# Splitting the first loads of a matmul with RMS norm over both hardware DMA queues, with the first PSUM moves on two engines and 8 warm-up matmuls

## The chip, the cores and the metric

The kernel runs on one core of one Trainium2 chip. The metric is the device time of one execution in microseconds; a median over several executions is given. Each comparison was made with runs of the kernel before on the same chip.

The engines of the core are PE (TensorE, matmul), DVE (VectorE), ACT (ScalarE), POOL (GpSimd) and SP (the sync engine). SP and ACT each issue on a hardware DMA queue; GpSimd issues on a software queue. All queues feed the same 16 DMA engines.

## The reference

```python
# a: 2048 x 2048, b: 2048 x 2048, gamma: 2048, all fp32
x = np.matmul(a, b)
rms = np.sqrt(np.mean(x ** 2, axis=-1, keepdims=True) + eps)
return (gamma * x / rms).astype(np.float32)
```

## The kernel before

A head of four row blocks of A (512 rows) is computed with plain matmuls while B streams in; the other row blocks use a Strassen-like scheme with seven products on B's sums. The contraction has 16 tiles of 128, taken in 8 pairs. Pair 0 is loaded in fp32 on the hardware queues and cast on chip; pairs 1 to 7 come on GpSimd's queue, which casts to bf16 on the way (fp32 read, bf16 written). "B tile 0" and "B tile 1" below are the two tiles of pair 0.

```python
nc.sync.dma_start(out=a0f, in_=a[0:HB * P, 0:W2].rearrange("(r p) k -> p r k", p=P))   # A of pair 0
for t in range(2):                                                                     # B tiles 0 and 1
    nc.scalar.dma_start(out=b0f[t], in_=b[t * P:(t + 1) * P, 0:HALF])
# ...
def load_head(kp):                       # a later pair: its A, then its B
    nc.gpsimd.dma_start(out=ah(kp), in_=a[0:HB * P, kp * W2:(kp + 1) * W2].rearrange(...))
    load_b(0, kp)
# ...
load_head(1)
identity_f = consts.tile([P, P], FP32, name="identity_f")
make_identity(nc, identity_f)
for kp in range(2, 4):
    load_head(kp)
# ...
for _ in range(11):                      # warm-up matmuls on zeros
    nc.tensor.matmul(warm_bank, warm[:, 0:P], warm[:, 0:CH], start=True, stop=True)
# ...
def transpose_first():
    # eight fp32 transposes of A's pair 0 into two PSUM banks, then:
    for t in range(2):
        cast_first = [lambda: nc.vector.tensor_copy(out=raw[0][0][:, t, :CH], in_=b0f[t][:, :CH]),
                      lambda: nc.scalar.copy(out=raw[0][0][:, t, CH:], in_=b0f[t][:, CH:])]
        move = [lambda h=h: nc.vector.tensor_copy(
            out=head_at[:, t, 2 * h:2 * h + 2, :], in_=view[t][:, 2 * h:2 * h + 2, :])
            for h in range(2)]
        for work in (cast_first + move if t == 0 else move + cast_first):
            work()
# ...
for kp in range(KP):                     # the head: 14 matmuls of 512 columns a pair, 8 transposes, 2 more
    # loads of a later pair; transposes of pair kp + 1; matmuls of pair kp
```

In pair 0 PE does 7 matmuls on tile 0, 5 on tile 1, the transposes of pair 1's A, and the last 2 on tile 1.

Of the kernel before, what the change touches and what calls it, by code (L numbers as in the profile page):

```python
# [17 lines left out]
def kernel(  # L18
# [13 lines left out]
    nc = tc.nc  # L32
    P = 128
    M, K = a.shape
    _, N = b.shape
    KT = K // P
    KP = KT // 2
    W2 = 2 * P
    MB = M // P
    CH = 512  # L40
    NCH = N // CH
    HALF = N // 2
    HB = 4
# [15 lines left out]
    head_at = consts.tile([P, KT, HB, P], BF16, name="head_at")  # L59
    raw = [[consts.tile([P, 2, HALF], BF16, name=f"b_{j}_{kp}") for kp in range(KP)]  # L60
           for j in range(2)]
# [4 lines left out]
    a0f = early[:, 0:2048].bitcast(FP32).rearrange("p (r k) -> p r k", r=HB)  # L66
    b0f = [early[:, 2048 + t * 2048:2048 + (t + 1) * 2048].bitcast(FP32) for t in range(2)]
# [21 lines left out]
        return (at_even, at_odd)[(mb // 2) % 2][:, mb % 2]  # L89


    nc.sync.dma_start(out=a0f, in_=a[0:HB * P, 0:W2].rearrange("(r p) k -> p r k", p=P))
    for t in range(2):
        nc.scalar.dma_start(out=b0f[t], in_=b[t * P:(t + 1) * P, 0:HALF])

    def ah(kp):
        return ah_slot[(kp - 1) % NAH]
# [36 lines left out]


    warm_bank = ps_a.tile([P, CH], FP32, name="acc")
    for _ in range(11):
        nc.tensor.matmul(warm_bank, warm[:, 0:P], warm[:, 0:CH], start=True, stop=True)

    gamma_sb = consts.tile([P, N], FP32, name="gamma_sb")  # L140
# [2 lines left out]
    def transpose_first():  # L143
        bank = [ps_t.tile([P, CH], FP32, name="tbank"), ps_a.tile([P, CH], FP32, name="acc")]
        view = [b.rearrange("p (r m) -> p r m", r=HB) for b in bank]
        for t in range(2):
            for r in range(HB):
                nc.tensor.matmul(view[t][:, r, :], a0f[:, r, t * P:(t + 1) * P], identity_f,
                                 is_transpose=True, start=(r == 0), stop=(r == HB - 1))
        for t in range(2):  # L150
            cast_first = [lambda: nc.vector.tensor_copy(out=raw[0][0][:, t, :CH],
                                                        in_=b0f[t][:, :CH]),
                          lambda: nc.scalar.copy(out=raw[0][0][:, t, CH:], in_=b0f[t][:, CH:])]
            move = [lambda h=h: nc.vector.tensor_copy(
                out=head_at[:, t, 2 * h:2 * h + 2, :], in_=view[t][:, 2 * h:2 * h + 2, :])
                for h in range(2)]
            for work in (cast_first + move if t == 0 else move + cast_first):
                work()

    def transpose_head(kp):  # L160
        bank = ps_t.tile([P, CH], FP32, name="tbank")
# [236 lines left out]
    for r in range(HB):  # L398
        x_tile(r, 0)
    transpose_first()  # L400
    for kp in range(KP):
        if kp + 4 < KP:
# [334 lines left out]
```

## Time and profile before

| | before |
|---|---|
| time, median of 3 runs | 224.7 us |
| span of the profiled run | 222.6 us |
| PE busy | 211.1 us, 95% |
| A of pair 0 landed | 6.43 us |
| B tile 0, tile 1 landed | 5.12, 8.67 us |
| B of pairs 1, 2, 3, 4 landed | 12.34, 16.04, 19.87, 24.65 us |

The landings are the times in the trace at which a load's semaphore was complete, from the span's start. First the page: the busy share of PE and its granted clock (what the trace records of the TensorE clock, as a share of full speed), both in tenths, in 40 slices of 5.6 us each.

```profile
PE   7899999999999999999999999999999999999950
...
PEclk9999999999999999999999999999999999999997
```

The chain of work that ended last, in order of time (start, duration, what), the lines that matter:

```profile
7.18 17.47 DMA b<-in_b_dram
24.64 0.04 issue
24.69 1.67 PE acc L350 x7
...
69.41 140.08 PE acc L279 x648
```

PE runs unbroken from 24.69 us to 209.5 us. Before that the chain is a load: the B of pair 4. So the length of the program is that landing, plus a fixed run of PE, plus a tail.

The timeline of the first pair (start, duration, engine, line, operation, how many; in brackets the idle time before it and what ended it):

```profile
5.14 0.62 ACT L153 CAST b<-early 128x512 bf16<-128x512 f32 x1 [2.17 <-DMA early<-in_b_dram]
5.14 0.73 DVE L151 CAST b<-early 128x512 bf16<-128x512 f32 x1 [1.32 <-DMA early<-in_b_dram]
...
7.03 0.60 PE L148 MATMUL acc<-identity_f,early 128*128 128x128 f32 x4
7.23 0.76 DVE L154 CAST head_at<-tbank 128x256 bf16<-128x256 f32 x2 [1.36 <-PE tbank L148]
7.71 2.76 PE L350 MATMUL acc<-b,head_at 128*128 128x512 bf16 x12
7.90 0.75 DVE L154 CAST head_at<-acc 128x256 bf16<-128x256 f32 x2
8.69 0.62 ACT L153 CAST b<-early 128x512 bf16<-128x512 f32 x1 [2.93 <-DMA early<-in_b_dram]
8.69 0.43 DVE L151 CAST b<-early 128x512 bf16<-128x512 f32 x1
...
12.38 0.81 PE L350 MATMUL acc<-b,head_at 128*128 128x512 bf16 x3
```

B tile 1 is cast at 8.69 us, just in time: the 12 matmuls starting at 7.71 us take 2.76 us without a break, 0.22 us apart. Pair 1 begins at 12.38 us, right after its B landed (12.34).

### The profile page before, as it was taken

To read this page: it belongs to the slowest core of one execution; us is meant where nothing else is said; L and a number is where in the kernel's file an instruction comes from. 1 tells how busy PE (TensorE), PEld (TensorE's weight loads), DVE (VectorE), ACT (ScalarE), POOL (GpSimd) and SP (SyncE) were. 2 spreads that over 40 slices of the span, in tenths; PEclk is the share of its full clock that TensorE was granted. 3 is DMA by queue.
4 is the path that set the end of the run, shared out by engine and by line. 5 is a ranking of instruction groups with operands and counts; after the bars stand their busy time and mean duration, and the time that the engine had idled before them with its cause. 6 is when DMAs were issued, how large, how long until landed. Compare 5 with 4: busy or idle time off the path is not lost.

```text
span 222.6 us, 3026 instructions
## 1 busy us (share of the span) xinstructions
PE 211.1 (95%) x1043; PEld 98.6 (44%) x1043; DVE 161.8 (73%) x324; ACT 129.1 (58%) x272; POOL 24.5 (11%) x49
## 2 busy tenths in 40 slices
PE   7899999999999999999999999999999999999950
PEld 2445444444454444444444444444444444444430
DVE  2427557983999989978949298837994589587692
ACT  3110002807698895799646985699478954334570
POOL 7534232300000001000100002000200000000000
PEclk9999999999999999999999999999999999999997
DMA  6999999999973499818889259945994794044045
GB/s 184 223 202 209 203 208 211 212 303 259 327 280 159 188 272 292 310 72 226 276 228 400 58 174 222 366 151 143 246 368 168 97 282 189 0 188 193 0 190 188
DMA packets 36176, 47.13 MB, mean 212 GB/s; under 512 B 21952, under 2 KB 26048, under 8 KB 34496
## 3 DMA queue, kind: packets, MB, share of 16 engines
q0 software_dynamic: 9648, 23.33, 41.6%
q1 hardware_dynamic: 26080, 22.29, 33.0%
q10 hardware_dynamic: 432, 1.31, 2.0%
q8 instruction: 8, 0.13, 0.2%
q14 instruction: 8, 0.07, 0.1%
HBM read 34.60 MB, written 16.78 MB: 231 GB/s over the span
## 4 chain that ended last, share of the span: by engine, by line
PE 83%; DMA 8%; DVE 2%; POOL 2%; issue 1%; ACT 1%; DVEq 0%; ACTq 0%; POOLq 0%
PE acc L279 63%; PE acc L350 18%; DMA b<-in_b_dram 8%; POOL early L106 1%; DVE x L617 1%; POOL b L100 1%; DVE x L620 1%; PE tbank L179 1%; PE tbank L382 1%; PE tbank L165 1%; ACT sq L291 0%; DVEq L732 0%; ACT sq L682 0%; DVE x L690 0%; DVE r L322 0%
## 5 line engine op out<-in xcount | busy, mean ns | idle before, releaser
L279 PE MATMUL acc<-b,s 128*128 128x512 bf16 x376 | 83.3, 379 | 0.0
L279 PEld LDWEIGHTS <-s 128*128 128x128 f16 x472 | 46.2, 98 | 55.7 <-DVE s L244 0.2
L350 PE MATMUL acc<-b,head_at 128*128 128x512 bf16 x240 | 55.1, 379 | 0.6 <-DMA b<-in_b_dram 0.4
L291 ACT ACTIVATE sq<-x 128x512 bf16<-128x512 f32 x62 | 39.1, 631 | 10.9 <-DVE x L520 5.1
L340 DVE SCALAR_TENSOR_TENSOR x<-x,r,gamma_sb 128x1024 f32<-128x1024 f32 x28 | 34.7, 1282 | 0.8
L209 ACT ACTIVATE sq<-a 128x1024 bf16<-128x1024 f32 x24 | 25.4, 1057 | 16.8 <-DMA a<-in_a_dram 16.4
L350 PEld LDWEIGHTS <-head_at 128*128 128x128 bf16 x240 | 22.9, 98 | 26.7 <-issue 1.1
L393 ACT COPY x<-acc 128x512 f32<-128x512 f32 x11 | 5.9, 591 | 25.1 <-PE acc L350 25.1
L231 ACT ACTIVATE head_at<-a,s 128x2048 f16<-128x2048 f32 x10 | 19.9, 1990 | 0.0
L279 PEld LDWEIGHTS <-at_even 128*128 128x128 f16 x96 | 9.4, 98 | 11.5 <-issue 0.4
L279 PEld LDWEIGHTS <-head_at 128*128 128x128 f16 x96 | 9.4, 98 | 11.3
L100 POOL DMA_DIRECT2D b<-in_b_dram x15 | 10.6, 708 | 16.0 <-DMA b<-in_b_dram 13.2
L217 DVE TENSOR_SCALAR s<-norm 128x1 f32<-128x1 f32 x12 | 1.8, 150 | 14.3 <-ACT norm L212 14.2
L244 DVE TENSOR_TENSOR s<-at_even 128x1024 f16<-128x1024 f16 x15 | 9.7, 684 | 2.8 <-DMA at_even<-head_at 2.8
L291 ACT ACTIVATION_READ_ACCUMULATOR sq<-x 128x1 f32 x62 | 11.7, 188 | 0.0
L279 PE MATMUL acc<-t_left,s 128*128 128x512 bf16 x48 | 11.3, 379 | 0.0
L279 PE MATMUL acc<-early,s 128*128 128x512 bf16 x48 | 11.3, 379 | 0.0
L279 PE MATMUL acc<-early,at_even 128*128 128x512 bf16 x48 | 11.0, 379 | 0.0
L279 PE MATMUL acc<-t_left,at_even 128*128 128x512 bf16 x48 | 10.9, 379 | 0.0
L509 ACT COPY x<-acc 128x512 f32<-128x512 f32 x10 | 5.7, 575 | 8.9 <-PE acc L279 8.9
L279 PE MATMUL acc<-t_left,head_at 128*128 128x512 bf16 x48 | 10.8, 379 | 0.0
L279 PE MATMUL acc<-early,head_at 128*128 128x512 bf16 x48 | 10.8, 379 | 0.0
(86 smaller groups left out, 205.8 us busy)
## 6 DMA issues: line engine op xcount, KB each, us to landing
out_dram<-x SPq DMA_DIRECT2D x30, 512.0 KB, 3.1
a<-in_a_dram POOLq DMA_DIRECT2D x12, 1024.0 KB, 8.5
b<-in_b_dram POOLq DMA_DIRECT2D x15, 512.0 KB, 17.1
early<-in_a_dram POOLq DMA_DIRECT2D x7, 256.0 KB, 14.8
early<-in_b_dram ACTq DMA_DIRECT2D x2, 512.0 KB, 5.9
gamma_sb<-in_gamma_dram POOLq DMA_DIRECT2D x1, 1024.0 KB, 19.9
out_dram<-x SPq DMA_DIRECT2D x3, 256.0 KB, 3.5
early<-in_a_dram SPq DMA_DIRECT2D x1, 512.0 KB, 5.7
```

The lines of the kernel that those rows point to most:

```text
L100: nc.gpsimd.dma_start(out=raw[j][kp], in_=b[kp * W2:(kp + 1) * W2, j * HALF:(j + 1) * HALF].rearrange("(t p) n -> p t n", p=P))
L106: nc.gpsimd.dma_start(out=ah(kp), in_=a[0:HB * P, kp * W2:(kp + 1) * W2].rearrange("(r p) k -> p r k", p=P))
L165: nc.tensor.matmul(view[:, t, r, :], ah(kp)[:, r, t * P:(t + 1) * P], identity, is_transpose=True, start=(t == 0 and r == 0), stop=(t == 1 ...
L209: nc.scalar.activation(out=junk, in_=a32[mb][:, h * HALF:(h + 1) * HALF], func=ACTF.Square, scale=2.0 ** -8, accum_out=n2[:, h:h + 1])
L231: nc.scalar.activation(out=a16[mb], in_=a32.pop(mb), func=ACTF.Copy, scale=factor.pop(mb))
L244: nc.vector.tensor_tensor(out=s_sum[s], in0=x, in1=y, op=op)
L279: nc.tensor.matmul(bank, lhsT[:, kp, :], rhs, start=(start and kp == 0), stop=(kp == KP - 1), skip_group_check=not start)
L291: nc.scalar.activation(out=sq[:, 0:CH], in_=src, func=ACTF.Square, scale=inv_sqrt_n, accum_out=msq[mb][:, c:c + 1])
L340: nc.vector.scalar_tensor_tensor(out=x, in0=x, scalar=r, in1=gamma_sb[:, h * HALF:(h + 1) * HALF], op0=ALU.mult, op1=ALU.mult)
L350: nc.tensor.matmul(bank, head_at[:, kt, r, :], head_rhs(c, kt), start=(kt == 0), stop=(kt == KT - 1))
L393: copy(out=x_chunk(*g), in_=banks[g])
L509: nc.scalar.copy(out=x21, in_=p2)
```

## The change

The intent: both hardware queues are busy with halves of the same loads, A first, since A has to be transposed before anything else; the moves of the transposed tiles go to VectorE for tile 0 and to ScalarE for tile 1, ahead of B's casts; and since A comes earlier, fewer warm-up matmuls are run ahead of it.

```diff
-    nc.sync.dma_start(out=a0f, in_=a[0:HB * P, 0:W2].rearrange("(r p) k -> p r k", p=P))
+    queues = (nc.sync, nc.scalar)
+    for h, queue in enumerate(queues):
+        queue.dma_start(out=a0f[:, 2 * h:2 * h + 2, :],
+                        in_=a[2 * h * P:(2 * h + 2) * P, 0:W2].rearrange("(r p) k -> p r k", p=P))
     for t in range(2):
-        nc.scalar.dma_start(out=b0f[t], in_=b[t * P:(t + 1) * P, 0:HALF])
+        for h, queue in enumerate(queues):
+            queue.dma_start(out=b0f[t][:, h * CH:(h + 1) * CH],
+                            in_=b[t * P:(t + 1) * P, h * CH:(h + 1) * CH])
 ...
-    for _ in range(11):
+    for _ in range(8):
         nc.tensor.matmul(warm_bank, warm[:, 0:P], warm[:, 0:CH], start=True, stop=True)
 ...
-        for t in range(2):
-            cast_first = [...]; move = [...]           # cut: as printed above
-            for work in (cast_first + move if t == 0 else move + cast_first):
-                work()
+        copy = (nc.vector.tensor_copy, nc.scalar.copy)
+        def move(t):
+            for h in range(2):
+                copy[t](out=head_at[:, t, 2 * h:2 * h + 2, :], in_=view[t][:, 2 * h:2 * h + 2, :])
+        def cast(t, h):
+            copy[h](out=raw[0][0][:, t, h * CH:(h + 1) * CH], in_=b0f[t][:, h * CH:(h + 1) * CH])
+        move(0); cast(0, 0); cast(0, 1)
+        move(1); cast(1, 0); cast(1, 1)
```

More of the change, by code (lines that the diff above doesn't have):

```diff
@@ L149, in transpose_first @@
                                  is_transpose=True, start=(r == 0), stop=(r == HB - 1))
-        for t in range(2):
-            cast_first = [lambda: nc.vector.tensor_copy(out=raw[0][0][:, t, :CH],
-                                                        in_=b0f[t][:, :CH]),
-                          lambda: nc.scalar.copy(out=raw[0][0][:, t, CH:], in_=b0f[t][:, CH:])]
-            move = [lambda h=h: nc.vector.tensor_copy(
-                out=head_at[:, t, 2 * h:2 * h + 2, :], in_=view[t][:, 2 * h:2 * h + 2, :])
-                for h in range(2)]
-            for work in (cast_first + move if t == 0 else move + cast_first):
-                work()
+        copy = (nc.vector.tensor_copy, nc.scalar.copy)
[4 more added lines that the diff above has]
+            copy[h](out=raw[0][0][:, t, h * CH:(h + 1) * CH], in_=b0f[t][:, h * CH:(h + 1) * CH])
+        move(0)
+        cast(0, 0)
+        cast(0, 1)
+        move(1)
+        cast(1, 0)
+        cast(1, 1)
     def transpose_head(kp):
```

## The prediction

> **What bounds the kernel now.** The page: span 222.6 us, PE busy 211.1 us (95%). The chain of waits in order of time: start-up and GpSimd's issues to 7.18 us; one load of B, 17.47 us, to 24.64 us; PE without a break from 24.69 to 209.5 us; a tail of 13 us. So the change pays only by moving the end of that load stream (PE waits 0.44 us there).
>
> Landings in the trace: first A 6.43 us, first B tiles 5.12 and 8.67 us; on GpSimd's queue B pairs 1 to 4 at 12.34, 16.04, 19.87, 24.65 us. PE needs 3.9 us for a pair, the stream about 3.8: lockstep. PE begins pair 1 at 12.38 us, just after its landing.
>
> Before 8.3 us the DMA engines are badly used. The hardware queues' 1.5 MB take from 1.81 to 8.34 us, 240 GB/s; later GpSimd's queue moves 206 GB/s as written, about 410 as read in fp32. Its first packet moves at 6.38 us, full rate comes near 8 us, as the hardware queues drain. From 6 to 8.3 us one hardware queue alone carries the second B tile, at about 222 GB/s.
>
> **What the change does.**
> - Loads: the same 1.5 MB, 768 KB on each hardware queue, A first; both stay occupied to the end. B's packets shrink from 4 KB to 2. The Trainium skill ("DMA: Bandwidth & Descriptors", Rules for kernel authors) says that spreading loads over issuers does not help bandwidth, as all share 16 engines. That holds where the engines are full; before 8 us they were not. Estimate: the hardware queues finish near 7.3 us (1.5 MB at 240 to 360 GB/s; the best half-microsecond was about 400). All later landings move forward by 1.0 us (0.3 to 1.4).
> - PE's start: A lands near 5 us; transposes (1.05 us) and moves (0.76 us for two) follow while B comes. First real matmul near 6.5 us, from 7.71. What exceeds the loads' shift is lost: PE waits at pair 1 (near 11.3) and pair 4 (near 23.6).
> - Moves: tile 1's go to ScalarE (two of about 0.4 us, an estimate from its 0.62 us cast of 512); VectorE loses 0.75 us. Off the critical path.
> - Warm-up: three matmuls fewer, 0.43 us each while cold; eight end near 4.9 us. The skill ("TensorE: Matmul & The Clock Gate", The HAM clock gate) ties full clock to about 3.4 us of activity; here weight loads quicken 2.9 us after the first matmul. Eight should just suffice.
>
> **Sum.** 224.7 - 1.0 = 223.7 us, range 222.9 to 224.6. Chances: faster by over 2% 0.01, within 2% 0.98, slower 0.01.
>
> **What would show it right.** First pair landed near 7.3 us, B pair 1 near 11.3, pair 4 near 23.6; PE's unbroken run starting near 23.7 and as long as before (185 us); PE's waits for B growing; tail unchanged.
>
> **What would make it wrong.** (a) 2 KB packets, or a gap after every load on a hardware queue (three each now), cost what balance gains: landings stay, 224.7. (b) GpSimd's queue starts by a latency of its own, not when the others drain. (c) Eight warm-ups don't always reach full clock: pair 0 runs at 0.43 us a matmul, against some 0.4 us of slack before pair 1. (d) Pair 4's late landing (4.8 us after pair 3) is an accident that falls elsewhere: up to 0.6 us either way.

## The result and the profile after

The changed kernel takes 227.12 us (median of 4, 226.97 to 227.54) against 224.61 us (median of 4, 224.16 to 224.71): the ratio is 1.0125, with a 95% interval of 1.0109 to 1.0142. It is 2.5 us slower; 1.0 us faster was predicted. Ratios here are the mean time of one kernel's fast runs over that of the other's of the same rounds, so they are not quite the ratio of the medians quoted. Executions over 1.5% slower than the fastest of the same kernel are left out of the means.

| | before | after |
|---|---|---|
| A of pair 0 landed | 6.43 | 3.93 and 4.20 us |
| B tile 0 landed | 5.12 | 6.29 and 6.76 us |
| B tile 1 landed | 8.67 | 10.39 and 10.64 us |
| B of pair 1, pair 4 landed | 12.34, 24.65 | 12.44, 23.91 us |
| GpSimd's first packet | 6.38 | 5.17 us |
| first matmul on tile 0, on tile 1 | 7.71, 9.23 | 6.79, 10.89 us |
| first matmul of pair 1, pair 4 | 12.38, 24.69 | 15.27, 26.97 us |
| first product of the second phase | 69.25 | 71.53 us |
| end of the span | 222.61 | 225.24 us |

The two landings in a cell are the two halves.

The same rows of the page, after:

```profile
PE   7399999999999999999999999999999999999950
...
PEclk9979999999999999999999999999999999999995
```

The chain after, in order of time:

```profile
1.79 8.85 DMA early<-in_b_dram
10.67 0.63 ACT b L162
11.34 1.86 PE acc L361 x4
13.20 0.85 PE tbank L176 x8
...
15.43 1.51 PE acc L361 x7
...
71.70 140.07 PE acc L290 x648
```

The chain no longer holds the B of pair 4. The load at its head is now one of the first pair, and PE runs unbroken from tile 1 on: 10.89 us. The second phase takes the same 140 us.

The timeline of the first pair, after:

```profile
4.62 0.60 PE L153 MATMUL tbank<-identity_f,early 128*128 128x128 f32 x4
5.06 0.60 PE L153 MATMUL acc<-identity_f,early 128*128 128x128 f32 x4
...
6.79 0.62 ACT L162 CAST b<-early 128x512 bf16<-128x512 f32 x1 [3.22 <-DMA early<-in_b_dram]
6.79 0.38 PE L361 MATMUL acc<-b,head_at 128*128 128x512 bf16 x1 [1.13 <-DVE b L162]
7.31 0.64 ACT L159 CAST head_at<-acc 128x256 bf16<-128x256 f32 x2
7.46 1.46 PE L361 MATMUL acc<-b,head_at 128*128 128x512 bf16 x6 [0.29 <-ACT b L162]
10.41 0.43 DVE L162 CAST b<-early 128x512 bf16<-128x512 f32 x1 [3.67 <-DMA early<-in_b_dram]
10.67 0.62 ACT L162 CAST b<-early 128x512 bf16<-128x512 f32 x1 [2.72 <-DMA early<-in_b_dram]
10.89 2.31 PE L361 MATMUL acc<-b,head_at 128*128 128x512 bf16 x5 [1.98 <-DVE b L162]
12.99 1.06 PE L176 MATMUL tbank<-identity,early 128*128 128x128 bf16 x8
```

PE starts 0.9 us earlier, finishes tile 0, and then waits 1.98 us for tile 1's cast, which waits for its load. And then it is slow: five matmuls take 2.31 us, so they are about 0.43 us apart, where before they were 0.22. Stretches of the profile show why: the columns are the stretch, its length, the busy time (and count) of PE, weight loads, DVE, ACT and POOL, then the granted clock, the DMA share and GB/s. Before, over 8 to 12 and 12 to 16 us:

```profile
8.00:12.00 4.00, 3.65 (x24) 1.83 (x23) 1.77 (x4) 0.62 (x1) 0.77 (x1) 1.00 1.23 204
12.00:16.00 4.00, 3.91 (x25) 1.92 (x24) 0.69 (x1) 0.59 (x1) 1.46 (x2) 1.00 1.25 205
```

After:

```profile
8.00:12.00 4.00, 1.95 (x8) 0.64 (x6) 0.43 (x1) 0.62 (x1) 0.77 (x1) 0.90 1.18 229
12.00:16.00 4.00, 3.99 (x19) 2.03 (x18) 0.69 (x1) 0.53 (x1) 1.47 (x2) 0.67 1.24 205
```

The granted clock is 1.00 in both stretches before, and 0.90 and 0.67 after: the trace's clock records put the half clock at 11.2 to 14.6 us.

The bookkeeping by these times: tile 1 starts 1.66 us later (10.89 against 9.23), and from tile 1 to pair 1 takes 4.37 us, not 3.15. That makes 2.88 us at pair 1. Before, PE still had to wait for pair 4's late B (4.51 us from pair 3 to pair 4, where a pair takes 3.90); after, it comes too late to wait, so 0.6 us are given back, and 2.28 us remain. They are there unchanged at the second phase. At the end of the span it is 2.63 us: another 0.35 us is added in the tail.

### The profile page after: what moved, and what is told of

The parts are those of the page before. It is cut to its first block, busy times and chain, and to the rows that moved or that the text cites. A ratio compares the mean times of both kernels' runs of the same rounds, so it can differ in the third digit from the quotient of the medians.

```text
span 225.2 us, 3027 instructions
## 1 busy us (share of the span) xinstructions
PE 212.0 (94%) x1040; PEld 99.1 (44%) x1040; DVE 161.0 (71%) x322; ACT 129.5 (58%) x274; POOL 24.5 (11%) x49
## 4 chain that ended last, share of the span: by engine, by line
PE 89%; DMA 4%; DVE 2%; ACT 1%; ACTq 0%; issue 0%; DVEq 0%
PE acc L290 62%; PE acc L361 23%; DMA early<-in_b_dram 4%; PE tbank L393 2%; PE tbank L176 2%; DVE x L628 1%; DVE x L631 1%; PE tbank L190 1%; ACT sq L302 0%; DVEq L743 0%; ACT b L162 0%; ACT sq L693 0%; ACTq L98 0%; ACTq L94 0%; DVE x L701 0%
## 5 line engine op out<-in xcount | busy, mean ns | idle before, releaser
L361 PE MATMUL acc<-b,head_at 128*128 128x512 bf16 x240 | 56.8, 385 | 3.5 <-DVE b L162 3.1
L220 ACT ACTIVATE sq<-a 128x1024 bf16<-128x1024 f32 x24 | 25.3, 1056 | 15.9 <-DMA a<-in_a_dram 15.6
L404 ACT COPY x<-acc 128x512 f32<-128x512 f32 x11 | 5.9, 590 | 26.3 <-PE acc L361 26.3
L255 DVE TENSOR_TENSOR s<-head_at 128x1024 f16<-128x1024 f16 x15 | 9.8, 687 | 1.5 <-DMA head_at<-head_at 1.5
```

The source lines that it names most:

```text
L220: nc.scalar.activation(out=junk, in_=a32[mb][:, h * HALF:(h + 1) * HALF], func=ACTF.Square, scale=2.0 ** -8, accum_out=n2[:, h:h + 1])
L255: nc.vector.tensor_tensor(out=s_sum[s], in0=x, in1=y, op=op)
L361: nc.tensor.matmul(bank, head_at[:, kt, r, :], head_rhs(c, kt), start=(kt == 0), stop=(kt == KT - 1))
L404: copy(out=x_chunk(*g), in_=banks[g])
```

## The experiments

Theory 1: A's early landing lets GpSimd's queue in, which takes DMA engines from B tile 1, now the last load on both queues. Theory 2: the split loads are slow by themselves (2 KB packets, a gap after each of three loads). Theory 3: the loss is in PE's clock or in the moves. The table gives all runs. Times are of the profiled run; "half clock" is where the trace records it in the first 25 us (every trace, that of the kernel before too, has another over its last microseconds); landings are of the later half where a tile comes in two.

| run | first GpSimd packet | B tile 1 landed | pair 1 landed | half clock | ratio to before |
|---|---|---|---|---|---|
| before | 6.38 | 8.67 | 12.34 | none | 1 |
| after | 5.17 | 10.64 | 12.44 | 11.2 to 14.6 | 1.0125 |
| loads_only | 5.20 | 10.41 | 12.50 | 12.2 to 15.6 | 1.0077 |
| rest_only | 6.19 | 8.47 | 12.06 | 8.4 to 11.8 | 1.0033 |
| moves_only | 6.29 | 8.79 | 12.36 | none | 1.0003 |
| keep_warm | 5.33 | 10.09 | 12.40 | none | 1.0195 (flawed) |
| keep_warm2 | 5.15 | 10.75 | 12.13 | none | 1.0061 |
| pool_late | 9.54 | 7.54 | 16.30 | 17.5 to 20.9 | 1.0253 |
| pool_on_a | 6.73 | 7.55 | 14.28 | 14.6 to 18.0 | 1.0126 |
| b_rows | 4.25 | 11.59 | 12.81 | 7.7 to 14.5 | 1.0197 |
| b_first | 5.88 | 9.85 | 12.91 | none | 1.0025 |
| a_last | 6.79 | 7.01 | 12.91 | 9.0 to 12.5 | one look, 227.93 us |
| split_b1 | 6.37 | 8.80 | 12.38 | none | 0.9994 |
| three_lanes | 6.17 | 8.56 | 12.12 | none | 1.002 |

All runs gave correct results.

### loads_only: the new loads alone

```diff
 # the kernel before, with
-    # its load issues of pair 0
+    # the changed kernel's load issues of pair 0
```

> The kernel before with the new load issues alone: 11 warm-up matmuls and the old moves and casts stay. If the loss is in the loads (theories 1 and 2: the second B tile lands at 10.4 to 10.6 us in place of 8.67), this is as slow as the whole change: 226.8 to 227.5 us, second B tile landing near 10.5 us, PE falling to half clock before it. If eight warm-ups or the moves on two engines cost the 2.5 us (theory 3), this stays near 224.6 us.

It took 226.28 us (225.78 to 226.9) against 224.58, a ratio of 1.0077 (1.0049 to 1.0106). The landings came as expected and with them most of the loss, but the time is a little below the band: the loads are about 1.7 us of it. Eleven warm-ups did not save the clock here: it fell to half at 12.2 us, after PE's 1.91 us wait for tile 1. That is the one profiled run. The four times fall in two pairs, 226.71 (profiled) and 226.9 us against 225.78 and 225.85; the faster pair has a slightly higher mean granted clock (0.986 and 0.987 against 0.982 and 0.981), so it may have kept full clock, which no trace shows.

### rest_only and moves_only: the other parts

```diff
 # rest_only: the changed kernel with the old load issues
 # moves_only: rest_only with
-    for _ in range(8):
+    for _ in range(11):
```

> The changed kernel with the old load issues: only the moves on two engines and 8 warm-ups remain. Theories 1 and 2: 224.4 to 224.9 us, PE starting pair 4 at about 24.7 us as before. Theory 3 (clock lost by fewer warm-ups, or moves in the wrong order): 226 to 227 us with matmuls of pair 0 spaced 0.43 us.

> The kernel before with the new moves and casts alone (11 warm-up matmuls, old loads). The first matmul of pair 0 starts about 0.6 us later, since its B half is now cast after the moves of A. If the 0.9 us of the run without the new loads came from eight warm-ups (its clock fell to half from 8.4 to 11.8 us), this is 224.4 to 224.9 us with no half clock; if it came from the new order of moves and casts, 225.3 to 225.7.

rest_only took 225.5 us (224.92 to 225.85) against 224.58, ratio 1.0033 (1.0009 to 1.0057): between the two theories' bands. moves_only took 224.4 us (224.17 to 224.77) against 224.32, ratio 1.0003 (0.9989 to 1.0016): the moves and casts cost nothing that shows, though the first matmul starts 0.6 us later. The two differ only in three warm-up matmuls. The stretch of 8 to 12 us, in the columns given above, of rest_only:

```profile
8.00:12.00 4.00, 3.67 (x10) 1.36 (x10) 0.70 (x2) 0.89 (x2) 0.78 (x1) 0.57 1.24 205
```

and of moves_only:

```profile
8.00:12.00 4.00, 3.63 (x22) 1.81 (x22) 1.14 (x3) 0.89 (x2) 0.78 (x1) 1.00 1.24 206
```

Ten matmul records against 22 in the same busy time: with eight warm-ups PE idles from 5.06 to 6.52 us and 0.74 us more before pair 0, and the clock falls to half from 8.4 to 11.8 us. So eight were too few in this trace, with A at 6.4 us; they cost 0.7 us by the ratios, 1.1 by the medians. The two ratios come from different rounds and their intervals touch, so the size is uncertain.

### keep_warm and keep_warm2: filling PE's wait

```diff
             head_matmul(banks[g], *g, kt)
+            if groups is groups1 and kp == 0 and n == len(groups) - 1:
+                fill = ps_t.tile([P, CH], FP32, name="tbank")
+                for _ in range(9):
+                    nc.tensor.matmul(fill, warm[:, 0:P], warm[:, 0:CH], start=True, stop=True)
```

> The changed kernel with nine dummy matmuls (about 2 us at full clock) between the two tiles of pair 0, to fill PE's 2 us wait and keep its clock. If the half clock after that wait is a loss of its own, PE's run from 10.9 us takes about 1.3 to 1.5 us less and the time falls to 225.6 to 226.0 us; if the loss is the late landing alone, it stays at 227.1 us.

keep_warm lacked the condition on groups1, so the nine matmuls also ran at 42 us and cost 1.94 us there: 229.05 us, ratio 1.0195. It says nothing about the time; its trace did show full clock throughout and pair 1 at 13.5 us.

> The run with nine dummy matmuls, mended: in the first one they also ran a second time, at 42 us, for 1.94 us. Now they run once, in PE's 2 us wait of pair 0. In the first one the clock stayed full and pair 1 began at 13.5 us in place of 15.3. If the half clock is a loss of its own beside the late landing, the time is 225.0 to 225.6 us and PE reaches pair 4 near 25.2 us, not 27.0; if it is not, 227.1.

keep_warm2 took 225.79 us (225.35 to 225.96) against 224.32, ratio 1.0061 (1.0047 to 1.0075), just above the band. Only the wait was filled; the landings stayed (tile 1 at 10.75 us), the clock stayed full, and half the loss went. Its stretches, in the columns given above:

```profile
8.00:12.00 4.00, 3.83 (x18) 1.58 (x17) 0.43 (x1) 0.62 (x1) 0.81 (x2) 1.00 1.19 223
12.00:16.00 4.00, 3.60 (x28) 1.98 (x27) 0.69 (x1) 0.59 (x1) 1.47 (x2) 1.00 1.25 205
```

So the half clock is a loss of its own, of about 1.3 us (227.12 to 225.79; from different rounds, but the ratios say 1.4), beside the late landing.

When is the clock lost? Over the first 25 us of the traces the clock record changes only in whole steps of 3.41 us, which lie differently in every run. In the step before each half clock, PE had been idle (gaps over 0.15 us, added up) for 1.91 us in loads_only, 1.98 in the changed kernel, 2.07 in b_rows, 2.21 in rest_only, 2.30 in pool_late, 2.54 in pool_on_a and 2.85 in a_last. No other recorded step with full clock after it held more than 1.76 us. That one is in pool_late, where a gap of 1.94 us (9.88 to 11.82 us) fell across two steps and cost no clock. So where a wait falls decides with its length.

### pool_late and pool_on_a: GpSimd held back

```diff
-    load_head(1)
     identity_f = consts.tile([P, P], FP32, name="identity_f")
     make_identity(nc, identity_f)
-    for kp in range(2, 4):
+    wait_for(b0f[1][:, CH - 1:CH + 1])     # pool_on_a: wait_for(a0f[:, 1:3, 0]), and 11 warm-ups
+    for kp in range(1, 4):
         load_head(kp)
```

(wait_for is a tiny GpSimd copy that waits for the load; it touches both halves. Cut here: its tile and a later call of it become two columns wide.)

> The changed kernel with GpSimd's loads held back until the second B tile has landed, so that the hardware queues have the DMA engines to themselves. Theory 1 (GpSimd's queue, let in at 5.2 us, takes the engines from the second B tile): that tile lands by 7.3 to 8.3 us in place of 10.5. Theory 2 (2 KB packets and gaps after each of three loads make the hardware queues slow by themselves): it still lands after 9.5 us. The time itself: B pair 1 lands 1 to 1.5 us after 12.4 in both cases, so no gain over 224.6 is expected: 225 to 226.5 us.

> The changed kernel with GpSimd's first loads issued only once A has landed (4.2 to 4.5 us) and 11 warm-up matmuls: the hold ends earlier than in the run that held GpSimd back until the second B tile. Theory 1: GpSimd's first packet near 6 to 6.5 us, the second B tile at 8 to 8.8 us, PE without a long wait in pair 0 and at full clock, B pair 1 at 12.3 to 13.2; time 224.3 to 225.3 us. If the loss were inherent in the split loads, 226 to 227.

In both, B tile 1 landed at 7.5 us. ScalarE's casts of loads_only, which has the same loads and 11 warm-ups:

```profile
6.63 0.62 ACT L158 CAST b<-early 128x512 bf16<-128x512 f32 x1 [3.05 <-DMA early<-in_b_dram]
...
10.44 0.62 ACT L158 CAST b<-early 128x512 bf16<-128x512 f32 x1 [3.19 <-DMA early<-in_b_dram]
```

and of pool_on_a, with the wait that it bought:

```profile
6.14 0.62 ACT L162 CAST b<-early 128x512 bf16<-128x512 f32 x1 [2.58 <-DMA early<-in_b_dram]
...
7.58 0.62 ACT L162 CAST b<-early 128x512 bf16<-128x512 f32 x1 [0.27 <-DMA early<-in_b_dram]
...
14.33 2.05 PE L361 MATMUL acc<-b,head_at 128*128 128x512 bf16 x5 [2.27 <-DMA b<-in_b_dram]
```

This decides between theories 1 and 2: the split loads, 2 KB packets and all, are through by 7.5 us when GpSimd's queue is out of the way, as the prediction had said of them, and by 10.4 us when it is not. It says nothing yet on the other half of theory 1, that A's landing lets GpSimd's queue in. The times are no gain: 230.29 us (ratio 1.0253) and 227.72 us (1.0126; the four fast runs 226.52 to 227.84), both above their bands, because pair 1 then lands at 16.30 and 14.28 us. GpSimd issues its loads later, and they also run slower: in pool_on_a the 2 KB packets of GpSimd's queue that began between 10 and 12 us took 271 ns on average, where an undisturbed stretch shows 173 ns. GpSimd issues further loads one after another until 12.04 us there, but the packets that began from 12.1 to 13 us still took 311 ns, and the single issues of the kernel before at 10.00 and 13.85 us left its packets at 173. So the slowing is seen, and its cause stays open.

### b_rows: 4 KB packets

```diff
-            queue.dma_start(out=b0f[t][:, h * CH:(h + 1) * CH],
-                            in_=b[t * P:(t + 1) * P, h * CH:(h + 1) * CH])
+            queue.dma_start(out=b0f[t][h * 64:(h + 1) * 64, :],
+                            in_=b[t * P + h * 64:t * P + (h + 1) * 64, 0:HALF])
```

> The changed kernel, but each queue loads 64 whole rows of each B tile (4 KB packets) in place of a column half (2 KB packets). If the engines share by packets, the hardware queues get about twice the share against GpSimd's packets, and the second B tile lands near 9 to 9.5 us in place of 10.5, the time falling to 225 to 226 us. If packet size plays no part, it lands at 10.2 to 10.7 us and the time stays at 226.3 to 227.3.

Above both answers: tile 1 landed at 11.59 us and the time is 228.69 us (ratio 1.0197). GpSimd's first packet came at 4.25 us, the earliest of all. Larger packets gave no larger share; but splitting by partitions also changes which rows each queue brings, so this does not say what 2 KB or 4 KB alone would do.

### b_first, a_last, split_b1: the order of the split loads

```diff
 # the kernel before (11 warm-ups, old moves) with loads of pair 0 in this order
+    # b_first:  halves of B tile 0, halves of A, halves of B tile 1, on SP and ACT
+    # a_last:   halves of B tile 0, halves of B tile 1, halves of A
+    # split_b1: A on SP and B tile 0 on ACT as before; then halves of B tile 1 on both
```

> The kernel before (old moves, 11 warm-up matmuls) with all loads of the first pair split over both hardware queues, but in the order: first B tile, A, second B tile. [...]If A's packets hold GpSimd's queue back, its first packet now comes at 6 to 6.6 us, the second B tile lands at 8.2 to 9.3 us, PE keeps full clock, and the time is 224.0 to 225.0. If GpSimd's queue starts near 5 us whatever the order, the second B tile lands after 10 us and the time is 225.8 or more.

> As the run before it, but A behind both B tiles on both queues: a sharp test of what holds GpSimd's queue back. If it is A's packets: first GpSimd packet at 6.5 us or later, all of the first pair landed by 7.3 to 8 us, one time near 224.5 to 225.5. If GpSimd's queue starts by its own latency: first packet near 5 us, and A lands only after 9 us, 226 us or more.

> The kernel before with only the second B tile split by column halves over both hardware queues, behind A on one and behind the first B tile on the other. The wish behind the change, to have both queues busy to the end, without A coming early. If A's end lets GpSimd in (near 6.3 us), the second B tile lands at 7.8 to 8.8 us, and B pair 1 no earlier than 12.0: 224.2 to 224.8 us, no real gain.

b_first took 225.04 us (224.92 to 225.13) against 224.43, ratio 1.0025 (1.0011 to 1.0038). GpSimd's first packet came at 5.88 us, ahead of the end of A's packets (6.21); tile 1 landed at 9.85 us. That is between the two answers. (In the traces before it with GpSimd's early issue, its first packet came 0.1 to 1.3 us after A's last.) a_last was the sharp test and refutes the idea that A's packets hold GpSimd's queue back: its first packet came at 6.79 us in the middle of A's packets (5.48 to 9.36 us), and A landed at 9.75 us. GpSimd's first issue is at 1.25 us in all these runs, and its first packet comes between 4.25 and 6.8 us; what decides when stays open. A fixed latency from issue to first packet does not: after the later issues of pool_on_a (5.13 us) and pool_late (7.95 us) the first packet came within 1.6 us.

split_b1 is a draw: 224.36 us against 224.43, ratio 0.9994 (0.9981 to 1.0006). No version beat the kernel before.

### three_lanes: the tail

All six-load kernels end their span later after the last store than those with three or four hardware loads.

```diff
+    extra = consts.tile([P, 3, 32], BF16, name="extra")
+    for i in range(3):
+        nc.sync.dma_start(out=extra[:, i, :], in_=t_left[:, i, 0, 0:32])
```

> The kernel before with three small on-chip copies of 8 KB added on the sync queue near 20 us, off every path: it issues six hardware loads or copies ahead of the first store, as the changed kernel does, and not three. In all nine traces so far of kernels with six, the span ends 1.26 to 1.29 us after the last store has landed; in the four with three or four, 0.90 to 0.99 us: the sync engine then checks the DMA semaphores one by one, and which check the last store answers depends on how many transfers came before. If that count is the cause, the distance is 1.25 to 1.30 us here too and the time 224.6 to 225.0 us, about 0.3 over before on the same chip, with PE's stages at the same times as before. If it comes from the new loads in some other way, 0.95 to 1.0 us and no difference.

It took 224.77 us (224.67 to 224.95) against 224.43, ratio 1.002 (1.0007 to 1.0034), and the span ends 1.29 us after the last landing, as after the change; before, it is 0.96 us. The waits of the sync engine's queue at the program's end (total, times, longest), before:

```profile
SPq L732 <- DMA out_dram<-x: 2.6, 4, 0.9
```

after:

```profile
SPq L743 <- DMA out_dram<-x: 2.9, 2, 2.3
```

and in three_lanes:

```profile
SPq L735 <- DMA out_dram<-x: 2.9, 2, 2.3
```

At the end, SP checks the DMA semaphores in a fixed order, some 60 ns each. With three transfers more ahead of the stores, the last store falls on a semaphore that is checked fourth and not ninth. So the rest of the checks comes after the landing. That is 0.3 us of the 2.5, and it has nothing to do with the first pair.

## Why the prediction was wrong

- The frame was right: only the landings ahead of PE's unbroken run count, and nothing after that changed: the second phase is 140.07 us against 140.08. A landed early (4.2 us; "near 5" was said), the first matmul came at 6.79 us ("near 6.5"), and the moves are off the critical path (moves_only, 1.0003).
- The step that failed is this one: "the hardware queues finish near 7.3 us", so that "all later landings move forward by 1.0 us". They finished at 10.64 us, and pair 1 landed 0.1 us later than before. The estimate held for the hardware queues by themselves: 7.5 us in pool_late and pool_on_a. What it left out is that GpSimd's queue came in at 5.17 us and worked beside them. It had been assumed to start as they drain, as in the trace before; risk (b) named the doubt but put no price on it. The start did not wait for the drain, as (b) said, though not by a fixed latency either (3.0 to 5.5 us after the issue at 1.25 us).
- Behind it lies an amount that hardly moved. In every run in which GpSimd issued at 1.25 us, with six arrangements of the first pair, pair 1 landed between 12.06 and 12.91 us. Up to 12.2 us, the DMA packets had read 3.34 MB from HBM before and 3.41 MB after (GpSimd's packets counted twice, since they write half of what they read); over all runs with that early issue it was 3.14 to 3.46 MB. The change altered only who came last, and it put last B tile 1, for which PE waits first.
- Risk (a) of the prediction ("cost what balance gains: landings stay") described the landing of pair 1, but gave 224.7 us for it. It missed that the first pair itself can become the bound, and that PE's wait has a second price.
- That price was risk (c), the clock, but by another road. "Eight should just suffice" was wrong: eight cost 0.7 to 1.1 us with the old loads (rest_only against moves_only). With the new loads, eleven did not save the clock in the profiled run (loads_only), since it falls after the wait for tile 1. The half clock is about 1.3 us of the loss (keep_warm2).
- "Tail unchanged" was wrong by 0.35 us in the profile; three_lanes shows 0.33 of it (1.29 us after the last landing, against 0.96).
- Risk (d) came true and was worth nothing: pair 4 landed 0.7 us earlier, when PE was no longer waiting for it.

The parts don't add up exactly: loads_only (+1.7 us) and rest_only (+0.7 to 0.9) make 2.4 to 2.6 of the 2.5 us measured, but both contain a half clock, and only one is in the changed kernel.

## What to carry to other kernels

When several queues share the DMA engines, rearranging loads moves their order of landing more surely than their total: ask for each arrangement which tile lands last, and who waits for it first. A rate at which one queue ran beside others is no rate for a new mix; in particular, don't take the start of another queue from a trace in which the loads were arranged differently. In these traces a wait of PE near the start cost its length and, where PE was idle for 1.91 us or more of one clock step, a stretch at half clock besides (about 1.3 us here).

## What the Trainium skill lacked or had wrong

- "DMA: Bandwidth & Descriptors", Rules for kernel authors, says that spreading loads over issuers, or splitting one into two partition halves, does not help. The runs agree (pair 1 at 12.06 to 12.91 us in all arrangements with GpSimd's early issue; b_rows, which splits by partitions, 1.0197). The prediction set it aside on the ground that the engines were not full before 8 us. For the hardware queues alone that held (7.5 us in pool_late), for the landing of pair 1 it did not. How queues share an engine the page does say (Queues, rings and completion order: the engine takes the queues in turn, by packets); no run here settles whether it was so. What it lacks is a measured case of a software queue that starts beside two busy hardware queues: here first packets came 3.0 to 5.5 us after the issue at 1.25 us.
- The same page has no measured case like the slow stretch of GpSimd's queue in pool_on_a: 271 ns for a 2 KB packet against 173 (seen, cause open).
- "TensorE: Matmul & The Clock Gate", Why this matters for your kernels, asks for no idle gaps over some 3 us. Here gaps of 1.9 to 2.0 us (loads_only, after), and of 1.5 and 0.7 us in one window (rest_only), were enough for half clock, and one of 1.94 us was not (pool_late). The window of about 3.4 us that Part 1 of the page gives agrees: in the first 25 us every half-clock stretch lasted 3.4 us, or 6.8 in b_rows.
- No page that was read tells of the checks of DMA semaphores at the program's end, whose order made three unrelated transfers cost 0.3 us (three_lanes).
